# Sparse layer without parts in the memory's products, its transposes a step later, and an early branch count

## The chip, the cores and the metric

The kernel runs on one core of a Trainium2 chip. A time is the device time of one execution in microseconds. Each engine has its own instruction queue and works in order; the engines meet at semaphores. TensorE (PE, with PEld for its weight loads) multiplies into PSUM, VectorE (DVE) and ScalarE (ACT) work element by element, GpSimd (POOL) does small things, and SyncE (SP) issues the DMAs.

## What is computed

Two model blocks run one after the other on 256 tokens of width 1024, in float32. The first block has two layers of neighbourhood and differential attention. The second has two layers, and both have the same frame: projections, a mixer, a cross-attention over a memory of 256 rows, an output projection, a layer norm, a mixture of 16 experts, a second layer norm.

```python
xq = proj[..., -XA_WIDTH:].reshape(B, S, XA_HEADS, HEAD_DIM)
mkv = mem @ mem_w_kv[i]                      # 256 x 1024 by 1024 x 512: keys and values of the memory
mk = mkv[..., :XA_WIDTH].reshape(B, N_MEM, XA_HEADS, HEAD_DIM)
mv = mkv[..., XA_WIDTH:].reshape(B, N_MEM, XA_HEADS, HEAD_DIM)
xa = memory_cross_attention(xq, mk, mv).reshape(B, S, XA_WIDTH)
y = jnp.concatenate([mix, xa], -1) @ w_out[i]
x = layer_norm(DEEPNORM_ALPHA * x + y, ln_g[i, 0], ln_b[i, 0])
f = hier_moe(x, ...)                         # top-1 group, then top-2 experts within it
```

The mixer of layer 0 is sparse attention (`nsa_mixer`): 12 heads with a compressed, a selected and a window branch. With 256 tokens the selected and the window branch are both causal attention over all keys, so the kernel computes them with one mask and two softmaxes. The mixer of layer 1 is latent attention.

## The kernel before

**A flow of steps.** A layer up to its experts is written as a `Flow`: a list of steps, most of them one slice k (128 rows) of a projection. For step s, `run` first issues the weight split of step s+2, then what was put `before` s, then the products of step s, then what was put `after` s. This order, written out by hand, is the order of every engine's queue; no planner changes it.

**A projection in parts.** `Proj` multiplies float32 values with TensorE's faster fp32r type at nearly full precision. `split` (lines 134 and 135) makes two parts of a weight slice: ScalarE casts it to fp32r (high part), VectorE subtracts (low part). The input is split in the same way by `split_to` (lines 140 and 141). `mm` then issues three products for each output, high by high, high by low, low by high (line 253).

**The sparse layer.** Its flow has 48 steps of input projections, two steps of transposes of the memory (`memory_T`), eight of the memory's keys, eight of its values (both a `Proj` of 256 columns), and then the output projection. Beside them run six pairs of heads, one pair every four steps. For a pair that starts at step s:

- after s: scores of the second 128 queries (line 462), both branches; before s+2 their maxima (line 361, VectorE), before s+3 the exponentials (line 370, ScalarE), before s+4 the normalising (line 164, VectorE);
- after s+4 and s+5: `transpose1`, the transposes of these weights, one head each (line 1426, TensorE), copied out by ScalarE before s+6 and s+7 (line 1430);
- two steps behind: the scores of the first 128 queries, after s+2, normalised before s+6, transposed after s+6 (`transpose0`, line 1437), copied out before s+8;
- after s+9: `values` (lines 1453 and 1456); before s+11 the result is split for the output projection.

**The experts.** `moe` runs 16 experts for up to CAP = 64 tokens each. Their weights come through a ring and through free tiles of 8 and 4 KB a partition (`b8`, `b4`); a transfer is issued when a tile comes free. The last expert's down projection is made in four quarters, and each quarter's sum goes into the layer's result. Between the third and the fourth quarter's sum stands a branch: if any expert has more than 64 tokens, a loop over all experts computes the rest. The count `cnt` is ready early in the layer, at its step 9. With these inputs the branch skips the loop, in both layers. `values_load` (line 2534) reads the count into a register of each engine, and `tc.If` (line 2535) branches on it on each engine.

**The next layer** (`mla_layer`) makes the memory's keys and values too, with plain float32 products (`memory_kv`, lines 962 and 966), two key products and one value product at a time, between its other work.

Of the kernel before, what the change touches and what calls it, by code (L numbers as in the profile page):

```python
# [19 lines left out]
ENGINES = {mybir.EngineType.PE, mybir.EngineType.DVE, mybir.EngineType.Activation}  # L20

P = 128
S = 256
D = 1024
KD = D // P
# [3 lines left out]
CAP = 64  # L29
# [184 lines left out]
class Proj:  # L214
# [16 lines left out]
    def mm(self, k):  # L231
        nc, nt = self.E.nc, self.ncol // P
        if self.done == 0 and self.feature:
            self.ps = [self.E.bank("pj") for _ in range((nt + 1) // 2)]
        elif self.done == 0:
            ps = [self.E.bank("pj") for _ in range(1 + (self.ncol > S))]
            self.ps = ps if self.ncol > S else [ps[0][:, :S], ps[0][:, S:]]
        first, last = self.done == 0, self.done == self.nk - 1
        self.done += 1
        hi, lo = self.parts.pop(k)  # L240
        xh, xl = self.xT() if callable(self.xT) else self.xT
        for t in range(nt if self.feature else 2):
            c = slice(t * P, t * P + P)
            if self.feature:

                o = self.ps[t // 2].rearrange("p (t s) -> p t s", t=2)[:, t % 2]
                ops, begin = ((hi[:, c], xh[:, k]), (hi[:, c], xl[:, k]), (lo[:, c], xh[:, k])), first and t % 2 == 0
            else:
                o = self.ps[t][:, :self.ncol]
                ops, begin = ((xh[:, k, c], hi), (xh[:, k, c], lo), (xl[:, k, c], hi)), first  # L250
                begin = first and (t == 0 or self.ncol > S)
            for i, (a, b) in enumerate(ops):
                nc.tensor.matmul(o, a, b, start=begin and i == 0, stop=last and i == 2, skip_group_check=True)  # L253
        self.E.free(hi)
# [34 lines left out]
    def finish(self, flow, end, delays=(1, 2)):  # L289
        for i, d in enumerate(delays[:len(range(0, self.ncol, 256)) if self.feature else 2]):  # L290
            flow.before(end - 1 + d, self.out, i)

# [802 lines left out]
def nsa_layer(E, x, flow, norm, W):  # L1097

    nc, a, work, small = E.nc, E.a, E.work, E.small
    win = a["nsa_w_in"]  # L1100
    t = {}
# [116 lines left out]
    s = s0 + 14  # L1218
# [25 lines left out]
    def kv_out(br):  # L1244
        return lambda i, ps: nc.scalar.activation(t["kv", br][:, i], ps, AF.Copy, scale=norm.r[:, i:i + 1])
# [43 lines left out]
    def xq_out(i, ps):  # L1289
# [3 lines left out]
    ps = [Proj(E, src, ncol, lambda: norm.xT, out, feature)  # L1293
          for src, ncol, out, feature in (([(0, win[:, 768:1280])], 512, spread, True),
                                          ([(0, win[:, :384]), (384, win[:, 2304:2340])], 420, q_out(0), False),
                                          ([(0, win[:, 1280:1792])], 512, kv_out(0), False),
                                          ([(0, win[:, 1792:2304])], 512, kv_out(1), False),
                                          ([(0, win[:, 384:768])], 384, q_out(1), False),
                                          ([(0, win[:, 2340:2596])], 256, xq_out, True))]
# [5 lines left out]
    for br in range(2):  # L1305
        s = s0 + 26 + 7 * br
# [63 lines left out]
    for g in range(2):  # L1370
        s = s0 + 18 + 24 * g
# [17 lines left out]
    yT = []  # L1389
# [71 lines left out]
    for j in range(6):  # L1461
        ms = [Head(E, None, None, j, b, None) for b in range(2)]
        s = starts[2 * j] + (j == 5)
        for i in range(2):
            d = s + 2 - 2 * i
            flow.after(d, scores, ms, i)
            flow.before(d + 2, maxima, ms, i)
            flow.before(d + 3, exps, ms, i)
            flow.before(d + 4, normalise, ms, i, 6 * (j // 3) + j % 3)
        for b, m in enumerate(ms):  # L1470
            flow.after(s + 4 + b, transpose1, m)
            flow.before(s + 6 + b, transposed1, m)
        flow.after(s + 6, transpose0, ms)
        flow.before(s + 8, transposed0, ms)
        flow.after(s + 9, values, ms)
        flow.before(s + 11, lambda j=j: (E.split_to(yT[0], j, t["po", j]), E.free(t["po", j])))


    mkv, xq = [], []
# [4 lines left out]

    def memory_T(k):
        if k == 0:
            t["memT"] = E.new_T("memT")
        E.transposes(t["mem"], k, lambda ps: t.__setitem__(("mT", k), ps))

    def memory_parts(k):  # L1490
        ps = t.pop(("mT", k))
        E.split_to(t["memT"], slice(k, k + 2), ps)
        E.free(ps)

    def memory_out(which):
        def f(i, ps):
            if i == 0 and which == 0:
                m = E.b4((2, 512), "mkv")
                mkv.extend([*(m[:, j].rearrange("p (t s) -> p t s", t=2) for j in range(2)), m])
            nc.scalar.copy(mkv[0] if which == 0 else mkv[1][:, i], ps)  # L1500
        return f
# [5 lines left out]
    flow.steps += [(lambda: None, lambda i=i: [memory_T(4 * i + 2 * k) for k in range(2)]) for i in range(2)]  # L1507
    flow.before(e + 2, lambda: E.free(t["mem"]))
    for which in range(2):
        Proj(E, [(0, a["mem_w_kv"][0][:, S * which:S * which + S])], S, lambda: t["memT"], memory_out(which),  # L1510
             which == 0).add(flow, ahead=10)
    flow.before(len(flow.steps), lambda: E.free(*t["memT"]))
    flow.before(starts[11] + 2, lambda: E.free(*t["qT"], *t["KT"]))
    flow.before(starts[11] + 10, lambda: E.free(t["kv", 0], t["kv", 1], t["pcT"]))
    flow.before(starts[15] + 1, lambda: E.free(t["xq"]))
# [769 lines left out]
def moe(E, x, i, W, st, columns, sums, tail=None, overflow=True):  # L2285
# [3 lines left out]
    nc, a, small, tc = E.nc, E.a, E.small, E.tc  # L2289
# [55 lines left out]
    made = {}  # L2345
# [52 lines left out]
    with tc.manual_schedule(engines=ENGINES):  # L2398
# [53 lines left out]
        for k in range(4):  # L2452
            t, c = k % 2, slice(512 * (k // 2), 512 * (k // 2) + 512)
# [3 lines left out]
        ps, work = {}, ()  # L2457

        def split(c, t):
            made["fp"] = E.split(made["f"][:, t, 512 * c:512 * c + 512])  # L2460
# [20 lines left out]
        for s in range(16 * NE + 2):  # L2481
            W.step = s
            e, k = divmod(s, 16)
# [20 lines left out]
        Y.result2()  # L2504
        st = small.tile([P, 2, 4, 6], F32, name="st", tag="st4")
        quarters = {}

        def stats(q, t):
            nc.vector.bn_stats(st[:, t, q], ps[q // 2, t][:, S * (q % 2):S * (q % 2) + S])  # L2509
# [21 lines left out]


    if overflow:
        most = nc.values_load(made["cnt"][0:1, 0:1], min_val=0, max_val=S)
        with tc.If(most > CAP):
            with tc.For_i(0, NE, 1) as e:
                rows = lambda w, n_: (lambda v, k0, nk: nc.sync.dma_start(
                    v, w.rearrange("e k c -> (e k) c")[bass.ds(e * n_ + k0 * P, nk * P), :]
                    .rearrange("(k p) c -> p k c", p=P)))
                rows8 = lambda w: (lambda v, k0, nk: nc.sync.dma_start(  # L2540
                    v, w.rearrange("e k c -> (e k) c")[bass.ds(e * D, D), :]
                    .rearrange("(p k) c -> p k c", k=KD)[:, k0:k0 + nk]))
                sl = small.tile([P, 2, 1], F32, name="osl", tag="osl")
                ge = E.b4((P + 4,), "oge", F32R)
                nc.vector.tensor_copy(sl, slot[:, :, bass.ds(e, 1)])
                nc.vector.tensor_copy(ge[:, 2:2 + P], E.gates[:, 2 * NE:2 * NE + P])
                nc.vector.tensor_copy(ge[:, :2], E.gates[:, bass.ds(2 * e, 2)])
                nc.vector.tensor_copy(ge[:, 2 + P:], E.gates[:, bass.ds(2 * e + 2 * NE + P, 2)])
                for b in range(1, S // CAP):
                    nc.vector.tensor_scalar(sl, sl, -float(CAP), None, op0=OP.add)  # L2550
                    Dg = new_hots(1)
                    hots(Dg, sl, 0)
                    hots(Dg, sl, 1)
                    g = new_group(1)
                    xg, (new_dT, ga) = g[0], new_back(g, 1)
                    for out in itertools.chain(gather(E, made["xs"], Dg, xg), back(E, Dg, ge, 0, new_dT, ga)):
                        out()
                    Z = Expert(E, [], lambda w: None, xg, 0, lambda: ga[:, :1])
                    for w, k, c in ((wg, D, FF), (wu, D, FF), (wd, FF, D)):
                        p = E.wload(rows(w, k) if c == D else rows8(w), k, c)  # L2560
                        m = 1024 // c
                        Z.w.append([lambda k, p=p, o=o: p(o + k) for o in range(0, k // P, m)])
                    for s in range(8):
                        Z.mm(s)
                    Z.hidden()
                    for fn in (lambda: Z.down(0), lambda: Z.down(1), Z.result1, Z.result2):
                        fn()
                    for t in range(2):
                        for c in range(2):
                            add(c, t, g[1][0][:, 0], Z.y)  # L2570
                    E.free(Z.y, Dg, g[1][0], xg)
                E.free(ge)
            for q in range(2):
                for t in range(2):
                    stats(q, t)
# [141 lines left out]
```

## Time and profile before

| | us |
|---|---|
| median of 3 runs (lowest, highest) | 1029.16 (1028.06, 1031.38) |
| the profiled execution | 1031.01 |
| its span, first to last instruction | 1029.2 |
| TensorE busy | 992.5 |
| VectorE busy | 658.8 |
| ScalarE busy | 440.0 |

The table by stage cuts the span: the first block and the sparse layer's input projections up to about 365 us, the memory's products with the attention up to about 412, the output projection and the router up to 460, the experts of the first expert layer up to 680, the latent layer up to 800, the experts of the second up to the end. Times inside the span count from its first instruction. A busy TensorE means that a matmul was under way, at whichever clock was granted.

### The profile page before, as it was taken

The numbers are of one execution on the slowest core, as the hardware profiler recorded it, in microseconds if no ns is written. First come the engines' busy times: TensorE is split into PE (matmuls) and PEld (weight loads), VectorE is DVE, ScalarE is ACT, GpSimd is POOL, SyncE is SP. The second block draws the span as 40 slices with busy tenths as digits, with TensorE's granted clock in tenths as the row PEclk, the third lists the DMA queues.
The fourth block names the chain that finished last, engine by engine and source line by source line (L and its number), as shares of the span: only waits on it lengthen the run. The fifth ranks groups of instructions, "written<-read, shape, count | busy, mean of one in ns | idle before, by whom it ended". The sixth has DMA issues, their size and how long they took to land. (4 is left out here: it accounts for less than half of the span.)

```text
span 1029.2 us, 16197 instructions
## 1 busy us (share of the span) xinstructions
PE 992.5 (96%) x5673; PEld 647.2 (63%) x5673; DVE 658.8 (64%) x1852; ACT 440.0 (43%) x1094; POOL 19.0 (2%) x38
## 2 busy tenths in 40 slices
PE   8999999999999988999999999989999999999994
PEld 8898889978897766774333433368877443434332
DVE  6767876568877777748475545548885646454556
ACT  6556664556663567543212121134883321212121
POOL 1000000000100000000000000000000000000000
PEclk9999999999999999999999999989999999999998
DMA  8954665444666623889999999982698799999994
GB/s 298 374 152 144 203 197 184 144 127 119 184 197 214 174 87 121 292 344 327 355 409 409 409 409 409 393 309 87 206 349 320 256 332 410 375 409 409 409 406 149
DMA packets 110699, 285.64 MB, mean 278 GB/s; under 512 B 14160, under 2 KB 30864, under 8 KB 110352
## 3 DMA queue, kind: packets, MB, share of 16 engines
q1 hardware_dynamic: 110608, 284.50, 76.6%
q8 instruction: 49, 0.80, 0.3%
q14 instruction: 42, 0.34, 0.1%
HBM read 283.41 MB, written 1.05 MB: 276 GB/s over the span
## 5 line engine op out<-in xcount | busy, mean ns | idle before, releaser
L135 DVE TENSOR_TENSOR wsp<-w,wsp 128x512 fp32r<-128x512 f32 (+4 forms) x272 | 170.9, 643 | 66.3 <-ACT wsp L134 64.9
L2173 PE MATMUL eg<-wa,xg 128*64 128x512 f32 x776 | 208.7, 600 | 0.0
L253 PE MATMUL pj<-xTh,wsp 128*128 128x256 f32 x768 | 154.4, 291 | 1.1 <-ACT wsp L134 0.6
L134 ACT CAST wsp<-w 128x512 fp32r<-128x512 f32 (+4 forms) x272 | 148.5, 582 | 9.3 <-PE pj L253 8.7
L253 PEld LDWEIGHTS pj<-xTh,wsp 128*128 128x128 f32 x768 | 124.0, 192 | 8.1 <-issue 4.6
L2173 PEld LDWEIGHTS eg<-wa,xg 128*64 128x64 f32 x776 | 56.3, 136 | 89.2 <-issue 83.2
L253 PE MATMUL pj<-xTl,wsp 128*128 128x256 f32 x384 | 108.8, 283 | 0.0
L253 PE MATMUL pj<-wsp,xTh 128*128 128x512 f32 (+3 forms) x352 | 108.5, 389 | 0.0
L2183 DVE SCALAR_TENSOR_TENSOR z<-z,eg 64x512 f32<-64x512 f32 x32 | 21.7, 679 | 127.0 <-ACT z L2180 127.0
L2193 DVE SCALAR_TENSOR_TENSOR hq<-z,gall,eg 32x128 f32<-32x128 f32 x256 | 88.9, 347 | 4.4
L2213 PE MATMUL dn<-wa,hT 128*64 128x512 f32 x380 | 90.4, 592 | 0.0
L2173 PE MATMUL eg<-w,xg 128*64 128x512 f32 x248 | 83.5, 600 | 0.0
L253 PE MATMUL pj<-wsp,yTh 128*128 128x512 f32 x256 | 82.8, 404 | 0.0
L2180 ACT ACTIVATE z<-eg 64x512 f32<-64x512 f32 x32 | 18.9, 590 | 144.9 <-PE eg L2173 144.9
L2223 ACT CAST ys<-dn 64x512 fp32r<-64x512 f32 x60 | 34.8, 579 | 94.5 <-PE dn L2213 63.1
L253 PEld LDWEIGHTS pj<-xTl,wsp 128*128 128x128 f32 x384 | 73.7, 192 | 0.4
L253 PEld LDWEIGHTS pj<-wsp,xTh 128*128 128x128 f32 x352 | 62.8, 188 | 11.6 <-issue 2.5
L253 PE MATMUL pj<-wsp,xTl 128*128 128x512 f32 (+3 forms) x176 | 66.7, 379 | 0.0
L2213 PEld LDWEIGHTS dn<-wa,hT 128*64 128x64 f32 x380 | 27.3, 137 | 54.3 <-issue 51.4
L370 ACT ACTIVATE z<-z,mx 128x256 f32<-128x256 f32 (+1 forms) x104 | 48.1, 468 | 12.9 <-DVE mx L361 12.9
L253 PEld LDWEIGHTS pj<-wsp,yTh 128*128 128x128 f32 x256 | 45.8, 188 | 9.9 <-issue 1.9
L253 PE MATMUL pj<-wsp,yTl 128*128 128x512 f32 x128 | 50.2, 392 | 0.0
(418 smaller groups left out, 1458.0 us busy)
## 6 DMA issues: line engine op xcount, KB each, us to landing
wa<-moe_w_down_dram SPq DMA_DIRECT2D x100, 512.0 KB, 10.2
wa<-moe_w_up_dram SPq DMA_DIRECT2D x99, 512.0 KB, 10.1
wa<-moe_w_gate_dram SPq DMA_DIRECT2D x95, 512.0 KB, 9.3
w<-w_in_dram SPq DMA_DIRECT2D x64, 512.0 KB, 4.6
w<-moe_w_gate_dram SPq DMA_DIRECT2D x33, 512.0 KB, 10.1
w<-moe_w_up_dram SPq DMA_DIRECT2D x29, 512.0 KB, 9.9
w<-moe_w_down_dram SPq DMA_DIRECT2D x28, 512.0 KB, 10.2
w<-w_out_dram SPq DMA_DIRECT2D x24, 512.0 KB, 3.9
```

Of the source, the lines that this page charges most:

```text
L134: self.nc.scalar.copy(hi, src)
L135: self.nc.vector.tensor_sub(lo, src, hi)
L253: nc.tensor.matmul(o, a, b, start=begin and i == 0, stop=last and i == 2, skip_group_check=True)
L370: E.nc.scalar.activation(z[i], (src or z)[i], AF.Exp, bias=mx[:, i:i + 1], scale=1.0 if src else -1.0, accum_out=sm[:, i:i + 1])
L2173: self.E.nc.tensor.matmul(self.ps[b * CAP:b * CAP + CAP], self.xg[:, k, self.j], w, start=k == 0, stop=k == KD - 1, skip_group_check=True)
L2180: self.E.nc.scalar.activation(self.th, self.ps[:CAP], AF.Tanh, scale=0.5)
L2183: self.E.nc.vector.scalar_tensor_tensor(self.th, self.th, 1.0, self.ps[:CAP], op0=OP.add, op1=OP.mult)
L2193: self.E.nc.vector.scalar_tensor_tensor(self.hq[32 * q:32 * q + 32, :, h], th[:, q], self.gate()[r], u[:, q], op0=OP.mult, op1=OP.mult)
L2213: self.E.nc.tensor.matmul(self.pd[n * CAP:n * CAP + CAP], self.hT[:, k], self.w[2][k](0)[:, 512 * n:512 * n + 512], start=k == 0, stop=k == 3,
L2223: self.E.nc.scalar.copy(self.y[r, n], self.pd[r])
```

## The change

Four edits go together.

1. `PlainProj` replaces `Proj` for the memory's keys and values in the sparse layer: no weight split, one plain float32 product for each output, both outputs in one PSUM bank.
2. The memory's transposes are copied out once, in float32, into one tile (`memT`) in place of two parts.
3. Both `transpose1` of a pair are issued after step s+5, and what follows them (copy, `transpose0`, its copy, `values`, the split of the result) one step later than before.
4. In `moe` the count is read behind the last but one expert's result and ahead of the last expert's four quarters. At that place a branch hint is marked for TensorE, VectorE and ScalarE; its value is 0 where the count is at most CAP. The `tc.If` carries the hint's label.

```diff
+class PlainProj(Proj):
+    def split(self, k):
+        pass
+
+    def mm(self, k):
+        if self.done == 0:
+            ps = self.E.bank("pj")
+            self.ps = [ps] if self.feature else [ps[:, :S], ps[:, S:]]
+        self.done += 1
+        w, x = self.w(k), self.xT()[:, k]
+        for t in range(2):
+            c = slice(t * P, t * P + P)
+            o = self.ps[0].rearrange("p (t s) -> p t s", t=2)[:, t] if self.feature else self.ps[t]
+            a, b = (w[:, c], x) if self.feature else (x[:, c], w)
+            self.E.nc.tensor.matmul(o, a, b, start=self.done == 1 and t == 0, stop=self.done == self.nk,
+                                    skip_group_check=True)
...
-        for b, m in enumerate(ms):
-            flow.after(s + 4 + b, transpose1, m)
-            flow.before(s + 6 + b, transposed1, m)
-        flow.after(s + 6, transpose0, ms)
-        flow.before(s + 8, transposed0, ms)
-        flow.after(s + 9, values, ms)
-        flow.before(s + 11, lambda j=j: (E.split_to(yT[0], j, t["po", j]), E.free(t["po", j])))
+        for m in ms:
+            flow.after(s + 5, transpose1, m)
+            flow.before(s + 7, transposed1, m)
+        flow.after(s + 7, transpose0, ms)
+        flow.before(s + 9, transposed0, ms)
+        flow.after(s + 10, values, ms)
+        flow.before(s + 12, lambda j=j: (E.split_to(yT[0], j, t["po", j]), E.free(t["po", j])))
...
-            t["memT"] = E.new_T("memT")
+            t["memT"] = E.b8((KD, S), "memT")
...
-        E.split_to(t["memT"], slice(k, k + 2), ps)
+        nc.scalar.copy(t["memT"][:, k:k + 2], ps)
...
-        Proj(E, [(0, a["mem_w_kv"][0][:, S * which:S * which + S])], S, lambda: t["memT"], memory_out(which),
+        PlainProj(E, [(0, a["mem_w_kv"][0][:, S * which:S * which + S])], S, lambda: t["memT"], memory_out(which),
...
         st = small.tile([P, 2, 4, 6], F32, name="st", tag="st4")
         quarters = {}
+        if overflow:
+            most = nc.values_load(made["cnt"][0:1, 0:1], min_val=0, max_val=S)
+            tc.mark_branch_hint_location(f"overflow{i}", hint=most // (CAP + 1), engines=sorted(ENGINES, key=str))
...
     if overflow:
-        most = nc.values_load(made["cnt"][0:1, 0:1], min_val=0, max_val=S)
-        with tc.If(most > CAP):
+        with tc.If(most > CAP, label=f"overflow{i}"):
```

## Rows read from the trace of the kernel before

**Rows 1.** The page: busy time and instructions of each engine; the queue of code transfers.
```profile
PE 992.5 (96%) x5673; PEld 647.2 (63%) x5673; DVE 658.8 (64%) x1852; ACT 440.0 (43%) x1094; POOL 19.0 (2%) x38
...
q8 instruction: 49, 0.80, 0.3%
```
**Rows 2.** Waits of TensorE: who for whom, total us, times, longest.
```profile
PE tp L1426 <- DVE z L164: 8.6, 5, 3.4
PE sum L2514 <- PEq L2535: 7.8, 2, 5.0
```
**Rows 3.** By stage: length, busy us (instructions) by engine, granted clock, DMA share.
```profile
350.00:370.00 20.00, 15.86 (x106) 12.45 (x106) 16.27 (x83) 14.08 (x50) 0.00 (x0) 0.83 0.37 104
370.00:390.00 20.00, 16.23 (x130) 12.07 (x128) 16.05 (x77) 13.61 (x52) 0.31 (x1) 0.98 0.36 111
390.00:410.00 20.00, 19.35 (x147) 14.87 (x144) 15.47 (x78) 14.44 (x51) 0.00 (x0) 0.94 0.35 120
```
**Rows 4.** Timeline, a long wait: start, duration, what [idle before, behind whom].
```profile
386.65 0.42 DVE L135 TENSOR_TENSOR wsp<-w,wsp 128x256 fp32r<-128x256 f32 x1 [1.24 <-ACT wsp L134]
...
388.73 0.41 PE L1426 MATMUL tp<-ident,z 128*128 128x128 f32 x2 [3.35 <-DVE z L164]
```
**Rows 5.** Timeline of TensorE, products of the memory's keys, starts six products apart.
```profile
384.03 0.40 PE L253 MATMUL pj<-memTh,wsp 128*128 128x256 f32 x2
...
384.74 0.40 PE L253 MATMUL pj<-memTh,wsp 128*128 128x256 f32 x2
```
**Rows 6.** Timeline of TensorE, the next layer's plain products of keys and values.
```profile
686.55 1.03 PE L962 MATMUL mkv<-memT,wkv 128*128 128x256 f32 x4
687.41 0.59 PE L966 MATMUL mkv<-wkv,memT 128*128 128x256 f32 x2
```
**Rows 7.** The memory's low part as a tile: shortest, median, longest ns; first and last start.
```profile
L141 DVE TENSOR_TENSOR memTl<-tp,memTh x4: 681/683/690, 366.8 to 371.9; 128x512 fp32r<-128x512 f32 x4
```
**Rows 8.** Line 2535, the branch of the first expert layer, by sequencer.
```profile
L2535 PEldq COMPARE_BRANCH  x1: 5677/5677/5677, 674.3 to 674.3; - x1
...
L2535 DVEq COMPARE_BRANCH  x1: 72/72/72, 675.5 to 675.5; - x1
```
**Rows 9.** The same line in the second expert layer.
```profile
L2535 PEldq COMPARE_BRANCH  x1: 3661/3661/3661, 1014.3 to 1014.3; - x1
```
**Rows 10.** Line 2534, the reads of the count.
```profile
L2534 PEldq TENSOR_LOAD <-cnt_i x2: 311/398/484, 673.7 to 1013.9; - x2
...
L2534 DVEq TENSOR_LOAD <-cnt_i x2: 318/430/543, 674.9 to 1015.1; - x2
```
**Rows 11.** Timeline around the first branch.
```profile
674.89 0.42 DVE L2251 TENSOR_TENSOR ys<-dn,ys 128x256 fp32r<-128x256 f32 x1 [0.58 <-ACT ys L2250]
...
680.12 1.19 PE L2514 MATMUL sum<-ys,dT 128*128 128x256 f32 x4 [5.02 <-PEq L2535]
```
**Rows 12.** Timeline around the second branch.
```profile
1015.12 0.42 DVE L2251 TENSOR_TENSOR ys<-dn,ys 128x256 fp32r<-128x256 f32 x1 [0.59 <-ACT ys L2250]
...
1018.16 0.71 PE L2514 MATMUL sum<-ys,dT 128*128 128x256 f32 x4 [2.83 <-PEq L2535]
```
**Rows 13.** Behind the first branch: length, TensorE busy, granted clock, DMA share, GB/s.
```profile
680.00:686.00 6.00, 5.88 (x24) 0.50 0.69 197
```
**Rows 14.** Timeline behind it: the end of the layer norm, and its first transposes.
```profile
685.62 0.80 ACT L1586 ACTIVATE x<-sum,mr,rs_r 128x512 f32<-128x512 f32 x1
...
690.44 0.60 PE L159 MATMUL tp<-ident,x 128*128 128x128 f32 x4
```
**Rows 15.** Timeline of TensorE, the last expert's quarters: first and last of seven rows.
```profile
1008.43 1.95 PE L2241 MATMUL dn<-wa,hT 128*64 128x256 f32 x16 [1.41 <-issue]
...
1014.60 0.73 PE L2514 MATMUL sum<-ys,dT 128*128 128x256 f32 x4
```
**Rows 16.** By stage, the first expert layer (columns of rows 3; last: GB/s).
```profile
460.00:470.00 10.00, 10.00 (x48) 4.40 (x49) 5.99 (x21) 2.44 (x8) 0.00 (x0) 1.00 0.52 161
510.00:520.00 10.00, 10.00 (x50) 3.31 (x48) 5.00 (x12) 1.75 (x3) 0.00 (x0) 1.00 1.03 411
```

More of the change, by code (lines that the diff above doesn't have):

```diff
@@ L1509, in nsa_layer @@
     for which in range(2):
-        Proj(E, [(0, a["mem_w_kv"][0][:, S * which:S * which + S])], S, lambda: t["memT"], memory_out(which),
+        PlainProj(E, [(0, a["mem_w_kv"][0][:, S * which:S * which + S])], S, lambda: t["memT"], memory_out(which),
              which == 0).add(flow, ahead=10)
-    flow.before(len(flow.steps), lambda: E.free(*t["memT"]))
+    flow.before(len(flow.steps), lambda: E.free(t["memT"]))
     flow.before(starts[11] + 2, lambda: E.free(*t["qT"], *t["KT"]))
```

## The prediction

> **What bounds the kernel now.** I read the page first: TensorE is busy in 96% of the span [rows 1], so a gain must come from the few microseconds in which it stands, from a lower clock, or from fewer columns. The view of waits for TensorE names the two large ones: 8.6 us in five waits at line 1426, the transposes of the last-128-query weights, behind VectorE's normalising (line 164), and 7.8 us in two waits behind its own sequencer at line 2535, the overflow branch of the two expert layers [rows 2]. The change touches both. Third, the table by stage: from 350 to 410 us TensorE is busy 51.4 of 60 us, so the 8.6 us stand here, and the granted clock is 0.83, 0.98 and 0.94 in the three stretches [rows 3]. The clock lies at its lower level (1.2 of 2.4 GHz) for some 3 us behind each of the three long waits; (0.17+0.02+0.06) x 20 us = 5.0 us are lost that way. In the same 60 us VectorE works 47.8 us and ScalarE 42.1. So the stretch is bound by TensorE except where it waits for VectorE, and a wait costs more than its length.
>
> How a wait comes about: a pair of heads takes four flow steps. VectorE normalises the second-block rows in step s+4, and TensorE transposes head 0 at the end of the same step. Ahead of that VectorE has the subtraction of a weight split (line 135), which waits until ScalarE, busy with exponentials, has made the cast: at 386.65 it had stood 1.24 us for it, and TensorE came to its transpose 3.35 us too early [rows 4].
>
> **The products without parts.** Keys and values of the memory are 2 x 8 x 2 = 32 outputs of 256 columns. Today each takes three fp32r products; six of them lie between the starts at 384.03 and 384.74, so 0.71/6 = 0.12 us each and 0.36 us for three [rows 5]. The next layer makes the same products in plain float32: the two key products of one k (four records, two a product) start at 686.55 and the next product at 687.41, 0.43 us each [rows 6]. The price on TensorE is 32 x (0.43 - 0.36) = +2.2 us, on the path, since TensorE is what is full here. Against it VectorE loses 16 split subtractions of 0.42 us [rows 4] and four subtractions of 0.68 us for the memory's transposes [rows 7], 16 x 0.42 + 4 x 0.68 = 9.4 us; ScalarE loses 16 casts (its copies of the transposes stay). And with the splits goes VectorE's coupling to ScalarE's queue that made the wait at 386.65. The weights are now read by TensorE at their own step, two steps later than by the split, so their four ring tiles come free some 5 us later; a DMA share of 0.35 to 0.37 here [rows 3] hides that, at its worst as a late load of an output weight (512 KB). One large tile less for the memory lets expert weights in earlier, under the same cover.
>
> **Transposes one step later.** Nothing is added; in step s+4 TensorE now has the scores of the next pair and a projection step ahead of the transposes. The slack grows by a step. With five rounds of four steps in what would be 48.6 us (below) that is 2.4 us, against waits of up to 3.4 us, of which the removed splits take another 1 to 2. The three long waits and their clock should go. What is late next is VectorE: the stretch would shrink from 60 to 60 - 8.6 - 5.0 + 2.2 = 48.6 us, in which VectorE has 47.8 - 9.4 = 38.4 us of work, 79%, unevenly: while the query features are still being made (350 to 370) it is at 81% already, and the splits that go there are few. I leave 2.0 us of waits. Values and their evacuation move a step too; the last pair's land at step 71, and the output projection asks for that part at 75. The z tiles are held a step longer (three buffers, two in use): VectorE may then wait for a transpose at the next pair's scores; the chain from there round (four maxima, four exponentials, four scalings) is some 5 us in a round of 9, so I cost it at nothing.
> Sum for the stretch: -8.6 - 5.0 + 2.2 + 2.0 = **-9.4 us**. Ends: 0 (all waits come back, the fp32r saving eaten) and -11.4.
>
> **Early count and prefetch.** Of the engines, only TensorE pays for the branch: COMPARE_BRANCH takes 5.68 us on it, 0.07 on VectorE [rows 8], and 3.66 us in the second expert layer [rows 9]. What TensorE waits to do there, the last quarter's sum, has its operand from VectorE at 674.89 + 0.42 = 675.31, but starts at 680.12 [rows 11]; in the second layer 1015.54 against 1018.16 [rows 12]. If the branch costs next to nothing, 4.7 and 2.5 us go. In the first layer there is more: from 680 to 686 TensorE is busy 5.88 us at clock 0.50 [rows 13], behind an idle stretch of 5.0 us; behind the second, 2.83 us, the row shows none. Without that idle time the work of these 6 us takes 3 us. It is memory transposes and products, TensorE's own queue, full up to 690.44, when it transposes the new x [rows 14]; x was ready at 686.42, so VectorE's chain has 4 us to spare and gets nearly all of its shift; I hold back 0.3. So 4.7 + 3.0 - 0.3 + 2.5 = **-9.9 us**.
> The trace of before shows no hint. Its cost is bounded by the branch of VectorE (0.07) and by a branch that still fetches (5.68, 3.66); I take the former, since about 100 instructions lie between hint and branch on TensorE (48 matmuls with as many weight loads from 1008.43 to 1015.3, seven rows, of which the first and the last stand) [rows 15], 6 us, above both fetches or close to them. The count's read takes 0.3 to 0.5 us on TensorE's sequencer [rows 10]. It now stands behind the last-but-one expert's products and ahead of the last's, where TensorE waits 1.41 us for the hidden values anyway [rows 15]; ScalarE and VectorE stand there too, or read under a running instruction. Uncovered it would be up to 0.5 us a layer; I take 0.1 for both. SP's read, of the same kind, comes ahead of four loads of the next layer's weights, whose first use lies behind the branch; that covers it.
>
> **Sum.** -9.4 - 9.9 + 0.1 = -19.2 us. The profiled execution took 1031.0 (span 1029.2 and 1.8 around it), which gives 1011.8; the median of the runs, 1029.2, lies 1.85 below it, so I forecast **1010.0**. Alone its range is 1006 to 1014: all waits gone and a microsecond of scatter, or twice the waits that I left and a partly covered fetch.
>
> **The rivals.**
> 1. *The hint is without effect.* Every 16 KB of code is a transfer of its own (49 for 11,346 instructions of TensorE, one per 232) [rows 1], and both branches fetch on demand, 5.68 and 3.66 us [rows 8, 9]. If code is fetched strictly in order, a hint can't change that. Then 4.7, 3.0 and 2.5 stay, less some 0.5 us a layer for the count's read that no longer stands ahead of the branch: 1029.2 - 9.4 - 1.0 = 1018.8. Chance 0.20.
> The Trainium skill, "Runtime: NRT & Kernel Launch", section "Instruction fetch mechanics", speaks for it: it calls prefetch purely sequential, and a taken branch out of the window a fetch before execution can go on. By that rule the time is this rival's, by the rows' short branches it is the forecast; that TensorE alone pays agrees with the rule only if its target alone is out of reach.
> 2. *VectorE becomes the bound* from 350 to 410. For: 79% in order, with exponentials in between; against: most of its waits were for the splits that go. Half of the 9.4 us then stays: 1010 + 4.7 = 1014.7. Chance 0.12.
> 3. *The expert weights don't come earlier.* The transfers run at their full 411 GB/s from 510 on [rows 16], and an expert layer that starts earlier may wait for them. Against: at 460 to 470 they ran at 0.52, waiting for free tiles, so they are bound to the steps and move with them. If half the shift were lost to waits: 1029.2 - 19.2/2 = 1019.6. Chance 0.09.
> 4. *Slower: the hint's fetch takes the place of the next piece of code.* Place: between hint and branch. It decides if a border of the 16 KB pieces falls into these 100 of 232 instructions, 0.43 a site: TensorE then finds its own next piece missing, and if the target is not kept either, pays twice: 5.7 + 3.0 and 3.7 more, 12.4 us, against 9.4 won: 1029.2 + 3.0 = 1032.2. For: the trace shows no target that was fetched ahead of its branch, so where such a fetch would find room is unknown; against: each piece of 232 instructions lasts some 20 us here, against a fetch of 4 to 6. Chance 0.05.
> 5. *Neither does what it says:* VectorE's normalising slips by the step that the transposes were given, and the branch fetches as before: the longer products cost 2.2 and the split waits that vanish give about as much back, 1029. Chance 0.04.
>
> **The numbers.** Forecast 0.50, rivals 0.20, 0.12, 0.09, 0.05, 0.04. The range holds the forecast's own and rivals 1 to 3: 1006 to 1020. A measurement of this kernel can tell about 0.3% (3 us) from no change. Faster by more: 0.91 (forecast and rivals 1 to 3); within: 0.05; slower: 0.04.
>
> **What would show it.** In the changed trace: the wait of line 1426 for line 164 down from 8.6 to 2 us or less and the clock at 1.00 through that stretch; 64 records of 0.43 us a pair for keys and values; COMPARE_BRANCH on TensorE below 0.3 us at both places, and no stretch at 0.50 behind the first. Still 3 us or more there is rival 1; a wait for another VectorE line is rival 2; TensorE waiting for DMA in the experts is rival 3; a stall between count and branch rival 4. The prediction is wrong in its core if the branch is cheap and the following work still runs at 0.50, or if the waits at 1426 come back elsewhere in the same stretch.

## The result

The changed kernel takes 1013.17 us (median of four executions, 1011.93 to 1016.16), the kernel before 1028.61 (median of four, the three of the table of before among them): ratio 0.9842, 95% interval 0.9807 to 0.9876. The forecast was 1010.0 in a range of 1006 to 1020. The profiled execution took 1012.07 (span 1010.3, mean granted clock 0.997), which is 18.94 below the one of before; the sum forecast between these two was 19.2. Between the medians it is 15.4. Both the agreement and the gap need explaining.

Page of the kernel after, busy time by engine, and the queue of TensorE's code transfers (before: [rows 1]):
```profile
PE 986.6 (98%) x5641; PEld 641.0 (63%) x5641; DVE 650.7 (64%) x1832; ACT 436.1 (43%) x1078; POOL 19.1 (2%) x38
...
q8 instruction: 48, 0.79, 0.3%
```
Its view of waits for TensorE, the rows of the two places (before: [rows 2]; the old line 1426 is now 1446, 2514 is 2538, the branch is 2558):
```profile
PE sc L482 <- DVE mx L381: 1.0, 1, 1.0
...
PE tp L1446 <- DVE z L164: 0.8, 3, 0.3
...
PE tp L1446 <- DVE qT L1306: 0.7, 1, 0.7
PE sum L2538 <- PEq L2558: 0.6, 2, 0.3
```
Its table by stage: the stretch of the memory's products [rows 3], and behind the first branch [rows 13]:
```profile
350.00:370.00 20.00, 17.98 (x142) 13.52 (x141) 15.85 (x87) 16.29 (x57) 0.31 (x1) 1.00 0.98 247
370.00:390.00 20.00, 19.52 (x130) 14.08 (x130) 15.31 (x85) 11.99 (x45) 0.00 (x0) 1.00 0.29 97
390.00:410.00 20.00, 20.00 (x131) 14.46 (x127) 17.57 (x72) 15.27 (x52) 0.00 (x0) 1.00 0.69 217
664.00:670.00 6.00, 5.70 (x43) 4.76 (x42) 3.51 (x12) 2.80 (x6) 0.70 (x1) 1.00 0.86 278
670.00:676.00 6.00, 6.00 (x32) 5.23 (x32) 2.32 (x5) 3.22 (x6) 0.00 (x0) 1.00 1.06 374
```
Of 8.6 us of waits at the transposes 1.5 are left, with 1.0 at the scores; the granted clock is 1.00 (its upper level) throughout, where it was 0.83, 0.98, 0.94, and behind the branch 1.00 for 0.50. Line 2558 by sequencer (before: [rows 8, 9]):
```profile
L2558 PEldq COMPARE_BRANCH  x2: 1516/1534/1552, 664.9 to 997.6; - x2
...
L2558 DVEq COMPARE_BRANCH  x2: 78/81/84, 666.2 to 998.8; - x2
```
Its timeline of TensorE: a piece of the memory's keys, then the last quarter's sum of each layer (before: [rows 5, 11, 12]):
```profile
370.99 1.03 PE L310 MATMUL pj<-memT,w 128*128 128x256 f32 x4
371.86 0.33 PE L1352 MATMUL pc<-ident,cmpT 96*128 96x96 f32 x2
...
666.66 0.71 PE L2538 MATMUL sum<-ys,dT 128*128 128x256 f32 x4 [0.30 <-PEq L2558]
...
999.28 0.71 PE L2538 MATMUL sum<-ys,dT 128*128 128x256 f32 x4 [0.26 <-PEq L2558]
```
TensorE's branch is shorter, 1.5 us, but not gone. The view puts 0.3 us of waiting to it in each layer, where it was 5.0 and 2.8. But in the first layer the branch ends at 664.94 + 1.55 = 666.49, and VectorE finishes the sum's operand only at 666.14 + 0.42 = 666.56, so the branch is covered by then:
```profile
666.14 0.42 DVE L2271 TENSOR_TENSOR ys<-dn,ys 128x256 fp32r<-128x256 f32 x1 [0.59 <-ACTq L2558]
```

Where the 18.9 us went, from the starts of the same instruction in both traces: the first product of the first expert layer 460.79 to 451.77, −9.0 (the stretch); the last quarter's sum there 680.12 to 666.66, another −4.7 behind the last quarter's products; the first transpose of the new x 690.44 to 674.13, another −2.8; the second layer's last sum 1018.16 to 999.28, another −2.6 behind its quarters. Between these places both traces keep step within 0.3 us. The first products of the experts before and after, and the first transpose after (the other rows are above or in [rows 11, 12, 14]):
```profile
460.79 2.79 PE L2173 MATMUL eg<-wa,xg 128*64 128x512 f32 x12
```
```profile
451.77 2.80 PE L2193 MATMUL eg<-wa,xg 128*64 128x512 f32 x12
...
674.13 0.60 PE L159 MATMUL tp<-ident,x 128*128 128x128 f32 x4
```

### The profile page after: what moved, and what is told of

It reads as the page before. It is cut to its first block, busy times and chain, and to the rows that moved or that the text cites. A ratio compares the mean times of both kernels' runs of the same rounds, so it can differ in the third digit from the quotient of the medians.

```text
span 1010.3 us, 16111 instructions
## 1 busy us (share of the span) xinstructions
PE 986.6 (98%) x5641; PEld 641.0 (63%) x5641; DVE 650.7 (64%) x1832; ACT 436.1 (43%) x1078; POOL 19.1 (2%) x38
## 5 line engine op out<-in xcount | busy, mean ns | idle before, releaser
L2193 PE MATMUL eg<-wa,xg 128*64 128x512 f32 x788 | 212.3, 600 | 0.0
L135 DVE TENSOR_TENSOR wsp<-w,wsp 128x512 fp32r<-128x512 f32 (+4 forms) x256 | 164.3, 656 | 59.5 <-ACT wsp L134 58.0
L134 ACT CAST wsp<-w 128x512 fp32r<-128x512 f32 (+4 forms) x256 | 142.2, 594 | 11.9 <-PE pj L253 8.7
L2233 PE MATMUL dn<-wa,hT 128*64 128x512 f32 x368 | 87.5, 592 | 0.0
L2200 ACT ACTIVATE z<-eg 64x512 f32<-64x512 f32 x32 | 18.9, 592 | 144.9 <-PE eg L2193 144.9
L2193 PE MATMUL eg<-w,xg 128*64 128x512 f32 x236 | 81.1, 600 | 0.0
```

Source lines behind the costliest of these rows:

```text
L134: self.nc.scalar.copy(hi, src)
L135: self.nc.vector.tensor_sub(lo, src, hi)
L2193: self.E.nc.tensor.matmul(self.ps[b * CAP:b * CAP + CAP], self.xg[:, k, self.j], w, start=k == 0, stop=k == KD - 1, skip_group_check=True)
L2200: self.E.nc.scalar.activation(self.th, self.ps[:CAP], AF.Tanh, scale=0.5)
L2233: self.E.nc.tensor.matmul(self.pd[n * CAP:n * CAP + CAP], self.hT[:, k], self.w[2][k](0)[:, 512 * n:512 * n + 512], start=k == 0, stop=k == 3,
```

## The experiments

Each kernel is the one before or the changed one with the edit named. Spans are of one profiled execution each.

### The stretch: each half alone, and both

`products` is the kernel before with `PlainProj` and the single `memT`; `later` the kernel before with the new steps of a pair; `flow` has both. The branch is the old one in all three.

```diff
# products (cut; also the class PlainProj and the single memT)
-        Proj(E, [(0, a["mem_w_kv"][0][:, S * which:S * which + S])], ...
+        PlainProj(E, [(0, a["mem_w_kv"][0][:, S * which:S * which + S])], ...
# later (cut; what follows moves one step on too)
-            flow.after(s + 4 + b, transpose1, m)
+            flow.after(s + 5, transpose1, m)
```


> The kernel before with the plain float32 products and the one memory tile alone; transposes and branch as before. Theory A (both edits of the stretch are needed: the splits hold VectorE up by 1 to 2 us at each long wait, the step in hand covers the rest): the five waits of the transposes for line 164 fall from 8.6 to about 4 us, the clock still falls behind the longest, +2.2 us of longer products: time about 3 us below before, 1025.5. Rival B (the splits and their waits for ScalarE are the whole cause): waits 2 us or less, clock 1.00 from 350 to 410, time about 9 us below before, 1019.5. Rival C (the splits are not the cause): waits as before, time 2 us above before, 1030.8.

> The kernel before with the transposes one step later alone; products in parts and branch as before. Theory A: waits of the transposes for line 164 down to about 2.5 us, little of the clock lost, no longer products: time about 8 us below before, 1020.5. Rival B (the splits are the whole cause): VectorE stays late by the splits, the waits stay above 5 us or stand at the next VectorE line: time 0 to 3 us below before, 1027. Rival D (the step alone does everything and the plain products only cost their 2.2 us): waits 2 us or less, clock 1.00, time about 11 us below before, 1017.5.

> The kernel before with plain products and later transposes together, branch as before. From the changed kernel's profile, where the stretch gave 9.0 us: time 9 us below before, 1019.5; if the two halves of the change acted on each other, this and the kernel with the early count alone do not add up to the changed kernel's 15.4 (medians) to 18.9 (profiled executions) us within a microsecond or two.

| | ratio to before (interval) | span |
|---|---|---|
| products | 0.9946 (0.9925 to 0.9967) | 1022.4 |
| later | 0.9969 (0.9954 to 0.9985) | 1024.7 |
| flow | 0.9931 (0.9907 to 0.9954) | 1021.9 |

By ratio, of 1030.8 us, that is −5.6, −3.2 and −7.1. In the profiled execution of `flow`, TensorE is 2 us late for a reason at the kernel's start (below); from there to the experts it gains 9.1 us, like the changed kernel. The two halves overlap: alone they sum to 8.8 by ratio, 11.7 by the stretch in their traces (6.4 and 5.3).

VectorE's waits from 350 to 410, in the kernel before, in `products`, in `later`:
```profile
DVE wsp L135 <- ACT wsp L134: 8.7, 6, 2.7
```
```profile
DVE wsp L135 <- ACT wsp L134: 0.4, 1, 0.4
```
```profile
DVE wsp L135 <- ACT wsp L134: 4.0, 4, 1.8
```
TensorE's waits at the transposes in `products` (timeline), and its longer waits in `later`:
```profile
354.99 1.09 PE L1446 MATMUL tp<-ident,z 128*128 128x128 f32 x4 [2.07 <-DVE z L164]
...
365.06 0.63 PE L1446 MATMUL tp<-ident,z 128*128 128x128 f32 x4 [1.61 <-DVE z L164]
```
```profile
358.34 0.59 PE L462 MATMUL sc<-KT,qT 64*128 64x256 f32 x5 [0.98 <-DVE mx L361]
365.05 1.09 PE L1426 MATMUL tp<-ident,z 128*128 128x128 f32 x8 [1.37 <-DVE qT L1286]
368.93 0.87 PE L1453 MATMUL po<-pT,kvs 128*64 128x256 f32 x8 [1.08 <-DVE mx L361]
...
386.56 0.63 PE L1426 MATMUL tp<-ident,z 128*128 128x128 f32 x4 [2.61 <-DVE z L164]
```
Without the splits the three later waits, among them the one of 3.35 us [rows 4], are gone; the first two, 2.07 and 1.61 us, stay, and go with the step in `flow`. With the step alone VectorE stays full (86.2 of 110 us busy from 340 to 450, against 78.9 in `products`), and TensorE waits for it at other lines too, longest (2.61 us) still at the old one: this is rival 2 of the prediction, in a kernel that keeps the splits. That both edits are needed, as theory A has it, the traces show (9.1 us against 6.4 and 5.3). The times say less: the intervals of `flow` and `products` overlap, though all five executions of `flow` (1021.65 to 1024.03) lie below all six of `products` (1024.16 to 1026.22). Theory A's sizes are wrong: the products were worth twice the 3 us it gave them, the step less than half of its 8. `products` takes away VectorE's work and its waits for ScalarE together, so what each of the two is worth stays open. Rival D (the step does everything and the products only cost) falls: adding the products to the step takes the ratio from 0.9969 to 0.9931.

### The branch alone

The kernel before with the count and the hint of the change.

> The kernel before with the early count and the hint alone. From the changed kernel's profile: TensorE's branch 1.5 us at both places in place of 5.68 and 3.66, no stretch at half clock behind the first, 7.5 us in the first expert layer and 2.6 in the second: time 10 us below before, 1018.5. Rival: part of the 7.5 us comes from the stretch's edits (another alignment of the code pieces): TensorE's branch stays at 3 us or more at one of the places, time 3 to 6 us below before.

0.9911 (0.9879 to 0.9944), −9.2 us; span 1020.2. Line 2538 is its branch, first and second expert layer:
```profile
L2538 PEldq COMPARE_BRANCH  x1: 1622/1622/1622, 674.0 to 674.0; - x1
...
L2538 PEldq COMPARE_BRANCH  x1: 1427/1427/1427, 1007.5 to 1007.5; - x1
```
From the experts on, the trace gains 9.4 us, the changed kernel's 9.9. The branch edit owes nothing to the stretch that these runs could show: 0.9911 x 0.9931 = 0.9843, the changed kernel's 0.9842, each with an interval of some 0.003 to either side. Its stretch is that of the kernel before, instruction for instruction, with the same waits (8.5 us), yet another clock than [rows 3]:
```profile
350.00:370.00 20.00, 15.86 (x116) 12.57 (x114) 16.44 (x83) 14.04 (x50) 0.00 (x0) 0.91 0.36 106
370.00:390.00 20.00, 16.23 (x136) 12.20 (x134) 17.39 (x85) 13.80 (x53) 0.31 (x1) 1.00 0.35 111
390.00:410.00 20.00, 19.37 (x144) 14.80 (x141) 15.29 (x78) 14.46 (x51) 0.00 (x0) 0.91 0.33 116
```
The loss is (0.09 + 0.09) x 20 = 3.6 us here, 5.0 in the profile of before: the same wait does not always bring the lower clock.

### What in the branch edit works: the read or the hint, and from where

```diff
# no_hint: the count is read early, no hint
-            tc.mark_branch_hint_location(f"overflow{i}", hint=most // (CAP + 1), ...)
-        with tc.If(most > CAP, label=f"overflow{i}"):
+        with tc.If(most > CAP):
# hint_wrong
+            tc.mark_branch_hint_location(f"overflow{i}", hint=most // (CAP + 1) + 1, ...)
# hint_late: the mark ahead of X.quarter(3);  hint_early: count and mark ahead of Y.down(0)
```


> The changed kernel with the count read early, but without the hint. Theory H (the hint lets the target's code be fetched ahead of the branch): TensorE's branch takes 3.7 to 6.2 us again at both places, the half clock behind the first comes back, and the time stands with the kernel that has the stretch's edits alone, 7 us below before (0.993), not 15 to 16 below (0.984). Rival R (it was the count's read, now no longer ahead of the branch): the branch stays at about 1.5 us and the time at 0.984.

> The changed kernel with the hint's value raised by one, so that it announces the loop and not the skip. Theory H (the hint's value picks the code that is fetched): the loop's code is fetched or nothing is, TensorE's branch takes 3.7 us or more at both places, 0.993. Rival (the mark alone starts a fetch of the target, whatever its value): branch 1.5 us, 0.984.

> The changed kernel with the hint ahead of the last quarter, some 25 recorded instructions of TensorE ahead of the branch; the count is read where it was. In the changed kernel the hinted fetch started 45 recorded instructions ahead of the branch and 96 to 105 behind the hint, 9 to 10 us after it. Theory F (the fetch starts when the queue comes within some 45 instructions of the branch, and the hint must be there by then): the hint comes too late, branch 3.7 us or more, 0.993. Rival T (the fetch starts a fixed number of instructions or a fixed time behind the hint): the same here, which the early hint tells apart. Rival S (the hint starts the fetch itself): the fetch starts at the hint, branch about 2.5 to 3 us, 0.987.

> The changed kernel with count and hint ahead of the last but one expert's down products, some 32 products earlier. Theory F: the fetch starts at the same place, 45 instructions ahead of the branch, branch 1.5 us, 0.984 as the changed kernel. Rivals T and S: the fetch starts earlier by as much as the hint, the branch costs 0.1 us, and the last 0.3 us a layer of TensorE's wait behind it go too: 0.6 us less than the changed kernel.

| | ratio (interval) | executions, us | TensorE's branch, layer 1 / 2, us |
|---|---|---|---|
| no_hint | 0.9918 (0.9895 to 0.9942) | 1020.9 to 1023.0 | 6.45 / 3.59 |
| hint_wrong | 0.9924 (0.9899 to 0.9949) | 1021.0 to 1023.3 | 7.08 / 3.39 |
| hint_late | 0.9906 (0.9870 to 0.9941) | 1013.5, 1016.9, 1022.2, 1022.6 | 1.99 / 1.74 (in that of 1013.5) |
| hint_early | 0.9839 (0.9817 to 0.9862) | 1013.6 to 1014.0 | 0.39 / 0.45 |

The rows of `no_hint`, `hint_wrong` and `hint_early`, both layers in one (shortest, median, longest ns):
```profile
L2557 PEldq COMPARE_BRANCH  x2: 3587/5016/6445, 666.6 to 1006.3; - x2
```
```profile
L2558 PEldq COMPARE_BRANCH  x2: 3388/5234/7081, 664.9 to 1004.6; - x2
```
```profile
L2558 PEldq COMPARE_BRANCH  x2: 394/422/449, 666.9 to 999.5; - x2
```
And `no_hint` behind the first branch, where the lower clock is back:
```profile
673.00:679.00 6.00, 5.83 (x27) 5.70 (x28) 3.63 (x10) 2.94 (x6) 0.70 (x1) 0.61 1.07 375
```
Theory H holds: it is the hint, with the right value; the early read alone gives nothing that shows (0.9918 against the 0.9931 of `flow`). The hint's place matters, but none of the theories F, T and S on where the fetch starts fits. In the changed kernel's trace the 16 KB of the branch's target start 9 to 10 us behind the hint, 1.0 us ahead of the branch; with the late hint 1.1 us behind the hint (S), but half of that kernel's executions are as slow as without one (F; none of these was profiled). With the early hint the branch falls to 0.4 us in both layers. The 0.6 us that this was to save were not there: TensorE still stands 0.15 us at each last sum, where it stood 0.30 and 0.26, because the operand comes from VectorE no sooner; the times are 0.9839 against 0.9842.

What the branch waits for can be read from the code transfers of all 14 traces. In the 21 places where it took over 1 us, it ended 2.3 to 2.7 us behind the start of a 16 KB transfer, the target's. Without a right hint that transfer started behind the branch's own start, by 2.0 to 4.6 us in the first layer and 1.0 in the second; with one, between 1.1 us ahead and 0.7 us behind. In the seven places where the branch took 0.4 to 0.5 us, the transfer had started 2.4 us or more ahead of it.

### Why executions of one kernel differ

> The changed kernel once more, as the control of the scatter and for a second profile. Theory W (part of the scatter between executions of the same kernel is the first weight slice: in ten profiles of this study TensorE's first wait for the cast of line 134 lies between 0.58 and 2.19 us at 7 to 8 us, and where it is 1.3 us or more the granted clock of the first 20 us is mostly 0.85 to 0.94 and the work up to 355 us stands 1.7 to 2.0 us later): executions between 1011.5 and 1016, median 1013 to 1014, 0.984 of before. Rival: they lie within a microsecond of each other, and the spread so far came from the chip that was used.

`after_again` is the changed kernel unaltered: 0.9839 (0.9819 to 0.9858), executions 1011.94 to 1016.40. Its profiled execution was the longest, and shows where 4.3 us of scatter lie. Its table by stage at the start and behind the first branch, the branch, and the sum behind it:
```profile
0.00:10.00 10.00, 6.90 (x34) 6.29 (x35) 3.81 (x10) 5.47 (x11) 1.73 (x13) 0.90 0.79 267
10.00:20.00 10.00, 10.00 (x80) 10.00 (x80) 6.57 (x18) 6.90 (x17) 0.00 (x0) 0.93 0.92 293
...
670.00:676.00 6.00, 6.00 (x30) 5.62 (x29) 3.65 (x11) 4.12 (x7) 0.70 (x1) 0.72 1.07 375
```
```profile
L2558 PEldq COMPARE_BRANCH  x2: 460/1776/3092, 666.1 to 1002.0; - x2
```
```profile
669.37 0.72 PE L2538 MATMUL sum<-ys,dT 128*128 128x256 f32 x4 [1.84 <-PEq L2558]
```
At the start 1.2 us are lost with the clock. At the first branch the same hint at the same place brought the target late: the transfer started 0.7 us behind the branch's start, the branch took 3.09 us in place of 1.55, TensorE stood 1.8 us and 6 us followed at 0.72, 3.2 us in all. In the second layer it came early, and the branch took 0.46 us.

Three kernels take these away, singly and together. `warm_start` puts four warming products (products whose result nobody reads) at TensorE's wait for the first weights; `hint_early_again` is the early hint alone; `early_warm` has both.
```diff
     norm.transpose(2)
+    E.warm(4)
     flow.before(0, norm.parts, 2)
```


> The changed kernel with four more warming products (eight records) of TensorE between its first eight transposes and the first product, where it waits for the first weight slice. Theory W: the clock stays at 1.00 in the first 20 us, the first product comes at 7.2 to 8.3 us as before, nothing is added to the path but at most 0.5 us where the slice is early: executions between 1011.5 and 1013.5, median 1 us below the changed kernel's. Rival (the slice's lateness alone, without the clock, makes the scatter, or it lies elsewhere): spread and median as the changed kernel's, within 0.5 us.

> Both edits together: count and hint ahead of the last but one expert's down products, and the four warming products at the start. Theory V (two things scatter in the changed kernel: the start of the hinted fetch, between 72 recorded instructions ahead of the branch and some 18 ahead of it, worth up to 3.2 us in the first expert layer, and the clock of the first 20 us, worth up to 2 us): TensorE's branch 0.4 to 0.5 us at both places, clock 1.00 in the first 20 us, executions between 1011.5 and 1013, median 1012.0, 1.3 us below the changed kernel's. Rival (an earlier hint has only happened to hit well in four executions): some executions at 1015 or more, median as the changed kernel's.

> The early hint alone, once more. Theory V: TensorE's branch 0.4 to 0.5 us at both places in this profile too, executions between 1012 and 1014.5 by the scatter of the start alone, none at 1016. Rival: executions up to 1016 as in the changed kernel, TensorE's branch 1.5 us or more at one of the places.

| | ratio (interval) | five executions, us |
|---|---|---|
| after_again | 0.9839 (0.9819 to 0.9858) | 1011.94 to 1016.40, median 1013.38 |
| warm_start | 0.9837 (0.9815 to 0.9860) | 1011.64 to 1015.63, median 1012.27 |
| early_warm | 0.9841 (0.9826 to 0.9857) | 1012.36 to 1012.88, median 1012.61 |
| hint_early_again | 0.9848 (0.9831 to 0.9864) | 1012.35 to 1014.48, median 1013.45 |

`early_warm`, start and branch; then the branch of `hint_early_again`:
```profile
0.00:10.00 10.00, 7.80 (x40) 7.32 (x41) 3.01 (x8) 4.59 (x9) 1.72 (x13) 1.00 0.76 262
10.00:20.00 10.00, 10.00 (x86) 10.00 (x85) 7.45 (x20) 7.70 (x20) 0.00 (x0) 1.00 0.88 289
```
```profile
L2559 PEldq COMPARE_BRANCH  x2: 399/424/449, 665.9 to 998.5; - x2
```
```profile
L2558 PEldq COMPARE_BRANCH  x2: 399/1024/1648, 667.3 to 999.9; - x2
```
With both edits the spread is 0.5 us, with the early hint alone 2.1, with the warming products alone 4.0, with neither 4.5. That is what theory V says, but five executions do not prove a spread: the four of `hint_early`, the same kernel as `hint_early_again`, lie within 0.3 us. `warm_start` kept its clock at 1.00, yet one execution, not profiled, took 1015.63, above the range expected of it. The early hint is not strict either: in one of its three profiles the second layer's branch took 1.65 us. The median with both comes 0.8 us below the changed kernel's, too little for the intervals: perhaps a steadier kernel, not one shown to be faster.

## Why the prediction came out as it did

- **The stretch, −9.4.** Measured −9.0 between the profiled executions: 6.1 us of waits (2.5 left; I had left 2.0) and all 5.0 us of clock, less the longer products. Their price was right: in the timeline above, four records of line 310 take 371.86 − 370.99 = 0.87 us, 0.43 a pair.
- **What removes the waits.** Sum right, shares wrong. I gave the step 2.4 us of slack a wait and the splits "another 1 to 2". Alone, the splits' removal is worth 6.4 us in the stretch in spite of the 2.2 that the products cost, the step 5.3. VectorE lost 8.1 us of work (9.4 forecast), and as much again in waits for ScalarE's casts, 8.7 to 0.4 us in `products`. I had quoted one of these six waits and never summed them. And the story told from [rows 4] fits the later waits only: the first two, 2.1 us each, outlived the splits.
- **The branch, −9.9.** Measured −10.1 between the profiled executions (4.7 + 2.8 + 2.6). The step behind it failed: "I take the former", that is 0.07 us, "since about 100 instructions lie between hint and branch" on TensorE, "6 us, above both fetches or close to them". The branch took 1.5 us, 0.4 at best, and the hint stood 10 us ahead, not 6: the fetch does not start at the hint. It cost little only because the last sum waits for VectorE until 666.56 anyway, and the branch ended at 666.49. In `after_again` it ended later and cost, with the clock behind it, 3.2 us more. So "below 0.3 us" was wrong as a test, and a cover worked out from the hint's distance was no cover. The +0.1 us for the count's read shows nowhere: across it both traces keep step.
- **From the profiled execution to the median.** This carries most of the gap between 1010.0 and 1013.17. I took off 1.85 us because the profile of before lay above the median of three. Of 42 more executions of that kernel, run beside the experiments, the median is 1030.3 (1026.75 to 1033.22): the three had come out low, the profile was ordinary. The rest is scatter in the terms: in the kernel after, the branch (up to 3.2 us) and the start (up to 2); in the kernel before, the clock of the stretch (5.0 or 3.6 us). The shares of these in 15.4 against 18.9 are not settled, since only profiled executions show them. By the ratios (0.9842 and 0.9839, two timings) the change is worth 16 to 17 us of 1030, 2 to 3 less than the sum. That the sum met the profiled difference within 0.3 us is therefore partly luck: 1012.07 lies near the fastest of its kernel, and the profiled execution of `after_again` would have given 1031.01 − 1016.40 = 14.6.
- **Rival 1** (no effect of the hint) was wrong, and `no_hint` is what it would have looked like: 0.9918, or 1021.9 of 1030.3. The Trainium skill, "Runtime: NRT & Kernel Launch", "Instruction fetch mechanics", calls prefetch purely sequential; without a hint the runs agree (3.4 to 7.1 us at every branch), with a right one they do not: the target's transfer starts ahead of the branch in 15 of 16 places.
- **Rivals 2 and 5** did not come: 2.5 us of waits for VectorE are left, 0.8 of them behind the normalising. **Rival 3** did not come: from its first product to its last quarter each expert layer kept its shift within 0.3 us (−9.0 and −8.7; −16.3 and −16.3). **Rival 4** (the hint's fetch costs a piece of code): no stall between hint and branch shows, and the page counts 48 code transfers for 49.

## What to carry to other kernels

Where one engine waits for a second, sum what the second waits for in that stretch before giving it slack: here, taking away its split work and with it its waits for a third engine was worth more than a step of delay, though it made the first engine's work longer. A branch that skips a large body on the busiest engine can cost more than its own length, through the clock behind it; here a hint of the right value removed most of that, and it has to stand well ahead, because the fetch may start late. A sum made on one profiled execution forecasts another profiled execution; for the median, several executions of the kernel before are needed, and terms that hang on a clock state or a fetch carry their own scatter.

## What was not expected of the hardware

- TensorE's branch over the loop took 3.4 to 7.1 us without a right hint (12 places in six kernels), longer in the first layer (4.6 to 7.1) than in the second (3.4 to 3.7); with the hint 0.39 to 3.09 us (16 places in eight traces), most often near 0.4 or 1.5. VectorE's and ScalarE's took 0.05 to 0.08 us with or without.
- When the hinted code starts to come varies between executions of the same program: 1.0 us ahead of the branch and 0.7 us behind its start in two traces of the changed kernel's first layer. Counted from the hint it came 1.1 to 13.9 us later over all traces. In `hint_early`'s first layer it seems to have taken the place of the transfer at the border of the 16 KB pieces (no other lies between it and the branch). What starts it stays open.
- An idle TensorE does not always bring the lower clock. At the kernel's start, where it waits 0.6 to 2.2 us for its first weights, a wait of 2.2 us brought a mean granted clock of 0.90 to 0.93 over the first 20 us in two traces, one of 1.6 us 0.94 and 0.89 over its two halves, one of 1.3 us a piece of 10 us at 0.83, 0.85 and 0.90 in three; but one of 1.7 us brought none, nor did one of 1.2 us.
